# Two small constants move to a 96-byte pool at the top of SBUF, and every right-side pool starts 96 bytes lower

## The chip, the cores and the metric

The kernel runs on one core of a Trainium2 chip. The time is the device time of one execution in microseconds. The core has five engines that follow their own instruction lists and meet at semaphores: PE (TensorE, matrix products; its weight loads are listed apart as PEld), DVE (VectorE), ACT (ScalarE), POOL (GpSimd) and SP (SyncE, which here only issues DMAs). The on-chip memory, SBUF, has 128 partitions; a tile lies at the same byte address in each of its partitions. Products are collected in PSUM.

## The reference

One layer of a hybrid block over a sequence of 1024 tokens of width 1024, in float32: an input norm with a modulation, one wide input projection, a gated mixer (gMLP), a state-space mixer (SSD) with a short convolution, two output projections that are gated and merged, a last projection, a residual and a norm.

```
h = rms_norm(x, norm_w) * (1 + scale) + shift
gm_u, gm_v, gm_z, ssm_z, xbc, dt_raw, g_a, g_b = split(h @ w_in)          # 1024 x 11296
y_a = spatial_gating(gelu(gm_u), gelu(gm_v), ...) * silu(gm_z)
xs, bm, cm = split(silu(causal_conv(xbc)))
y_b = rms_norm_groups((ssd_scan(xs, softplus(dt_raw), ...) + xs * d_skip) * silu(ssm_z))
merged = sigmoid(g_a) * (y_a @ w_proj_a) + sigmoid(g_b) * (y_b @ w_proj_b)
out = rms_norm(x + gate * (merged @ w_out), final_norm_w)
```

## The kernel before

The products that need precision are made from operands split into a high and a low part of a 4-byte type (the profile prints it as f32 in a matmul and fp32r in a cast). One logical product is then three matmuls: high by high, high by low, low by high. Each of these matmuls takes 128 columns of weights and streams 512 columns past them. Where they occur, in order of time:

- **Input norm and first columns**, up to about 70 us: `first_products`, issued through the helper `mm` at line 76, results in `acc`.
- **Input projection**, about 70 to 930 us: `product` (line 556, its matmul at line 560). A 2x2 block scheme with seven products in place of eight (`pair`). Twelve matmuls in a row go to one PSUM bank; each has other weights than the one before it. The streamed operands are tiles of `hpool` (`b11`, `t1`, ...), the weights tiles of `wpool`.
- **SSD scan with the first output projection filled in**, about 930 to 1159 us: the SSD matmuls are plain float32 (`yi`, `yn`, `sp`, `pc`, `px`). Between them `proj_a` (line 1267) draws its matmuls, results in `pma`, six to twelve at a time; at the end a rest of them runs without SSD work in between. Each set of weights is used twice running, and the two uses go to two PSUM banks. All operands are tiles of `hpool`.
- **Second output projection**, about 1159 to 1325 us: `multiply` (line 1452, matmul at line 1459), 56 units of 12 matmuls in the order p1, p5, p2, p3, p6, p7, p4, eight units each. The streamed operands `bh` and `bl` are tiles of `hpool`. The weights (`p1a`, `p5a`, ...) come from `big` (line 1356), which takes tiles of the pools `p2r` and `p2q`. Three matmuls go to one PSUM bank, then three to the next. The operands of a unit are loaded six units ahead (`loads`) and made four units ahead (`operands`, lines 1419 to 1447) by ACT and DVE. SP issues the loads in an order that is written out, and waits before each until its tile is free.
- **Last projection**, about 1325 to 1402 us: `out_products` (matmul at line 1658). Its operands are placed by `place` (line 1474) in parts of `p2r`'s and `p2q`'s `sl` tiles or in `hpool` tiles, whichever is free. Some ten microseconds of norm, scaling and the last stores follow.

All instructions on PE are pinned in the order of the program; other engines' instructions are ordered by a scheduler when the kernel is built.

**Where tiles lie.** Pools are stacked from both ends of SBUF. Left, from low addresses: `const`, `hpool`, then `p0`, and after it `wpool` and `wspool`. Right, from the top down: `w4pool`, `gmpool`, `gxpool`, `prepool`, and for the later stages `p2r`, `p2x`, `p2q`. In the built program the right side ends at byte 229,344 of a partition, which is 96 above a multiple of 128. Its pools' sizes are multiples of 128 but for that of `gxpool`, the lowest of its stack, and so every tile of the pools named starts 96 above a multiple of 128, except in `gxpool`, whose tiles start at 64 or 0. `hpool` starts at 24,448 and its tiles and those of `wpool` all start at a multiple of 128. In the two projections at the end this gives, counted over the program's 512-column matmuls (start of the operand, modulo 128):

| matmul at line | count | streamed operand | weights |
|---|---|---|---|
| 560 | all | 0 | 0 |
| 76, `pma` | 384 | 0 | 0 |
| 76, `acc` | 108 and 36 | 0 and 96 | 0 |
| 1459 | 672 | 0 | 96 |
| 1658 | 53 | 0 | 0 |
| 1658 | 117 | 0 | 96 |
| 1658 | 147 | 96 | 96 |
| 1658 | 7 | 96 | 0 |

Of the kernel before, what the change touches and what calls it, by code (L numbers as in the profile page):

```python
# [8 lines left out]
F32 = mybir.dt.float32  # L9
# [7 lines left out]
P = 128  # L17
D = 1024
S = 1024
KT = D // P  # L20
NCH = S // P
NG = 8
# [13 lines left out]
def hybrid_kernel(  # L36
# [33 lines left out]
    def cst(shape, name, dt=F32):  # L70
        return const.tile(shape, dt, name=name, tag=name)

    pin = tc.keep_in_program_order

    def mm(acc, l, r, first=True, last=True):
# [35 lines left out]
    cwt = cst([P, P], "cwt")  # L111
    dtb = cst([P, NH], "dtb")
    abc = cst([P, NH], "abc")
    dskt = cst([P, 16], "dskt")
    dsk = cst([P, NH], "dsk")
    sc = cst([P, KT], "sc")
    dthq = cst([P, NCH * NH], "dthq")
    dde = cst([P, NCH * NH], "dde")
    nacs = cst([P, NCH * NH], "nacs")
    cd = cst([P, NCH * NH], "cd")  # L120
    ssq = cst([P, NG * NCH], "ssq")
    conv_wt = cwt.rearrange("p (k i) -> p k i", k=4)
    conv_bt = par2[:, 0:32]
    snw = par2[:, 32:48]
# [1670 lines left out]
```

## Time and profile before

| | |
|---|---|
| three runs | 1413.42, 1415.43, 1416.88 us (median 1415.43) |
| profiled execution, first to last instruction (its span) | 1412.0 us |
| profiled execution's own time | the page gives the span alone; the three runs lie 1.4 to 4.9 us above it |
| PE busy | 98% of the span |
| DVE, ACT, POOL busy | 75%, 56%, 15% |
| mean granted PE clock | 0.998 |

A row of a timeline gives the start, the time, the engine, the line and the operation with the tiles it writes and reads, and how many like instructions in a row it stands for. The end of a matmul is modelled in this profile, and matmuls overlap in it, so the pace of PE is read from starts: the difference of two rows' starts over the number of matmuls between them. A row of the chain of waits gives start, time and what held the end of the kernel at that moment. A row of a table by windows gives the window, its length, then busy time and number of instructions of PE, PEld, DVE, ACT and POOL, the granted clock, the DMA engines' busy share and GB/s.

### The profile page before, as it was taken

What the parts mean: (1) busy time and instruction counts of PE and PEld (TensorE: products, weight loads), DVE (VectorE), ACT (ScalarE), POOL (GpSimd) and SP (SyncE); (2) the same over time, 40 slices, a digit from 0 to 9 for tenths busy, and PEclk for the clock granted to TensorE, in tenths of its full rate; (3) what the DMA queues carried; (4) which work ended last, traced back from release to release, by engine and by line L of the source; (5) the groups of instructions that cost most, each with busy time, mean ns of one, the idle gap of its engine ahead of it and who ended that gap; (6) DMA issues with size and microseconds to landing.
All of it is one profiled execution on the core that took longest, in us unless ns stands there. A gap on an engine that the chain in (4) does not pass through costs nothing. (4 is left out here: it accounts for less than half of the span.)

```text
span 1412.0 us, 20661 instructions
## 1 busy us (share of the span) xinstructions
PE 1386.7 (98%) x7051; PEld 1147.0 (81%) x7051; DVE 1062.5 (75%) x1863; ACT 796.2 (56%) x1471; POOL 212.5 (15%) x208
## 2 busy tenths in 40 slices
PE   8999999999999999999999999999999999999997
PEld 7788888888888888887888888888888878777886
DVE  5686677767778899788888785388777767866866
ACT  6664575656656665555666555586766723322443
POOL 0000000000000011110100010027878830000001
PEclk9999999999999999999999999999999999999999
DMA  8552333343344667777675774498878759867903
GB/s 269 159 166 83 127 104 108 102 128 110 121 135 127 199 197 236 244 239 233 203 205 175 243 213 134 167 347 313 279 268 286 275 188 347 307 219 267 374 6 120
DMA packets 271918, 283.13 MB, mean 201 GB/s; under 512 B 14300, under 2 KB 222596, under 8 KB 271812
## 3 DMA queue, kind: packets, MB, share of 16 engines
q1 hardware_dynamic: 184548, 198.39, 44.0%
q10 hardware_dynamic: 87264, 83.41, 17.7%
q8 instruction: 56, 0.92, 0.3%
q14 instruction: 50, 0.41, 0.1%
HBM read 194.42 MB, written 87.33 MB: 200 GB/s over the span
## 5 line engine op out<-in xcount | busy, mean ns | idle before, releaser
L775 POOL TENSOR_TENSOR wog<-wog,gb 128x256 f32<-128x256 f32 x16 | 17.0, 1080 | 673.5 <-DMA wog<-in_w_out_dram 673.5
L989 ACT ACTIVATE dcy<-dcy,nacs 128x128 f32<-128x128 f32 x256 | 78.6, 389 | 15.2 <-POOL dcy L984 14.8
L984 POOL TENSOR_SCALAR_AFFINE_SELECT dcy<-dcy 128x1024 f32<-128x1024 f32 x32 | 35.0, 1094 | 138.2 <-ACT ea L981 134.6
L902 ACT ACTIVATE ac<-ac 128x1024 f32<-128x1024 f32 x32 | 33.9, 1060 | 25.9 <-DVE ac L900 25.8
L981 ACT ACTIVATE ea<-dcy 64x512 f32<-64x512 f32 x64 | 40.1, 626 | 14.7 <-DMA dcy<-acs_d 14.2
L76 PE MATMUL pma<-yh,wah 128*128 128x512 f32 x128 | 43.3, 419 | 0.0
L76 PE MATMUL pma<-yh,wal 128*128 128x512 f32 x128 | 42.6, 414 | 0.0
L1071 POOL TENSOR_TENSOR yz<-y,sl 128x512 f32<-128x512 f32 x32 | 41.5, 1296 | 1.1
L1009 DVE TENSOR_TENSOR dcy<-dcy,pc 128x1024 f32<-128x1024 f32 x32 | 38.9, 1216 | 2.9 <-PE pc L79 1.4
L1069 DVE TENSOR_TENSOR ym<-yn,ea 128x512 f32<-128x512 f32 (+1 forms) x32 | 19.9, 622 | 27.3 <-PE yn L76 27.3
L76 PE MATMUL pma<-yl,wah 128*128 128x512 f32 x128 | 40.2, 395 | 0.0
L1070 POOL TENSOR_TENSOR y<-y,ym 128x512 f32<-128x512 f32 (+1 forms) x32 | 36.6, 1143 | 12.0 <-DVE ym L1069 11.2
L76 PEld LDWEIGHTS yn<-sl,st 128*128 128x128 f32 x224 | 30.3, 190 | 7.0 <-POOL yz L1091 2.1
L76 PE MATMUL sp<-xe,bn 128*128 128x256 f32 x112 | 32.6, 408 | 3.2 <-DVE xe L1005 1.2
L900 DVE SCALAR_TENSOR_TENSOR ac<-c2x,cwt,ac 128x1023 f32<-128x1023 f32 (+2 forms) x24 | 31.2, 1299 | 5.8 <-ACT ac L898 5.7
L1398 DVE SCALAR_TENSOR_TENSOR yn<-yn,par,rb 128x512 f32<-128x512 f32 x32 | 23.9, 748 | 15.0 <-DMA yn<-yb_d 14.6
L76 PE MATMUL yi<-dcy,xd 128*64 128x128 f32 x512 | 35.0, 279 | 0.0
L76 PE MATMUL yn<-sl,st 128*128 128x128 f32 x224 | 31.3, 276 | 3.6 <-DVE st L1039 3.6
L900 DVE SCALAR_TENSOR_TENSOR ac<-c2cb,cwt,ac 128x1023 f32<-128x1023 f32 (+2 forms) x24 | 31.2, 1299 | 4.4 <-ACT ac L898 4.3
L1673 POOL TENSOR_TENSOR r<-r,fnw 128x512 f32<-128x512 f32 x2 | 2.6, 1300 | 209.3 <-DMA out_dram<-r 209.3
L1037 POOL TENSOR_TENSOR st<-st,cd 128x256 f32<-128x256 f32 x48 | 32.5, 678 | 8.2 <-PE yn L76 5.1
L900 DVE SCALAR_TENSOR_TENSOR ac<-c1cb,cwt,ac 128x1023 f32<-128x1023 f32 (+2 forms) x24 | 31.1, 1296 | 1.4 <-ACT ac L898 1.4
(2977 smaller groups left out, 4404.0 us busy)
## 6 DMA issues: line engine op xcount, KB each, us to landing
sl<-s_d SPq DMA_DIRECT2D x32, 768.0 KB, 4.7
s_d<-ac ACTq DMA_DIRECT2D x32, 512.0 KB, 4.2
dcy<-acs_d SPq DMA_DIRECT2D x32, 512.0 KB, 9.0
aw<-in_ada_w_dram SPq DMA_DIRECT2D x16, 512.0 KB, 3.7
wbr<-in_w_proj_b_dram SPq DMA_DIRECT2D x64, 128.0 KB, 4.4
wb_d<-wbb ACTq DMA_DIRECT2D x32, 256.0 KB, 4.9
wb_d<-wbc ACTq DMA_DIRECT2D x32, 256.0 KB, 4.1
yb_d<-yz ACTq DMA_DIRECT2D x32, 256.0 KB, 5.3
```

Source lines behind the costliest of these rows:

```text
L76: pin(PE.matmul(acc, l, r, start=first, stop=last))
L900: V.scalar_tensor_tensor(ac[:, s:], cc[:, : S - s], conv_wt[:, 3 - s, i : i + 1], ac[:, s:], op0=ALU.mult, op1=ALU.add)
L902: A.activation(ac, ac, AF.Silu)
L981: A.activation(ea[hh * HD : (hh + 1) * HD], dcy.rearrange("p (j e) i l -> p e j (i l)", e=2)[hh * HD : (hh + 1) * HD, hh], AF.Exp)
L984: G.affine_select(out=d8, in_=d8, compare_op=ALU.is_ge, fill=-1e30, base=0, pattern=[[0, 2 * HPG], [1, P]], channel_multiplier=-1)
L989: A.activation(dcy[:, h, i, :], dcy[:, h, i, :], AF.Exp, bias=sub[:, i, h : h + 1])
L1009: V.tensor_tensor(d3, d3, pc[:, 0:256].unsqueeze(1).to_broadcast([P, HPG, 256]), op=ALU.mult)
L1037: G.tensor_mul(v3(s2), v3(self.st), fac(cd, g, s)[:, i].unsqueeze(2).to_broadcast([P, HPG, HD]))
L1069: V.tensor_tensor(m[:, :, t0:], yn.rearrange("p (j l) -> p j l", j=2)[:, :, t0:], ea[:, :, t0:], op=ALU.mult)
L1070: G.tensor_add(y1[:, :, t0:], y1[:, :, t0:], m[:, :, t0:])
L1071: G.tensor_mul(yz, y1, sl[:, 4:6])
L1398: V.scalar_tensor_tensor(t, t, snw[:, n : n + 1], rbs[n // 2, h], op0=ALU.mult, op1=ALU.mult)
```

## The change

Two constants, `dskt` (64 bytes in a partition) and `sc` (32 bytes), leave the left `const` pool and become a pool of their own, `edge`, the first on the right side. `edge` takes the topmost 96 bytes, so every other right-side pool starts 96 bytes lower: 229,248 is now their upper end, a multiple of 128. `ssq` on the left gets 24 unused columns (96 bytes), so that `hpool` and all left pools behind it stay where they were.

```
+    edge = ctx.enter_context(tc.tile_pool(name="edge", bufs=1, side="right"))
+    def edg(shape, name):
+        return edge.tile(shape, F32, name=name, tag=name)
...
-    dskt = cst([P, 16], "dskt")
+    dskt = edg([P, 16], "dskt")
     dsk = cst([P, NH], "dsk")
-    sc = cst([P, KT], "sc")
+    sc = edg([P, KT], "sc")
...
-    ssq = cst([P, NG * NCH], "ssq")
+    ssq = cst([P, NG * NCH + 24], "ssq")
```

In the built program all engines have the same instructions in the same order as before, the DMAs included. Addresses move: the tiles of the right-side pools from 96 to 0 modulo 128 (those of `gxpool` from 64 or 0 to 96 or 32), and between `dsk` and `ssq` the constants `dsk`, `dthq`, `dde`, `nacs`, `cd` and `ssq` move down by 64 or 96 bytes, from 0 (`dsk`: 96) to 32. All 512-column matmuls of lines 560, 1459 and 1658, of `pma` and of `acc` then have both operands at 0. Since tiles of successive pools overlap at other edges, three waits are not needed any more: two semaphores of the first mask at line 984, one of a state update at line 1037, and one of a scaling at line 1005 (all at the start of the SSD stage).

## The prediction

> **What bounds the kernel now.** I read the page first, then the chain of waits, and then the timeline of PE, because a PE that is always busy can only get faster by its own pace.
>
> ```profile
> span 1412.0 us, 20661 instructions
> PE 1386.7 (98%) x7051; PEld 1147.0 (81%) x7051; DVE 1062.5 (75%) x1863; ACT 796.2 (56%) x1471; POOL 212.5 (15%) x208
> ```
>
> PE works 98% of the span, DVE 75%. An address can matter to the time only through PE, through the short stretches where PE waits, or by slowing another engine by a quarter. The chain in order of time, for the stages in which the change moves operands of matmuls:
>
> ```profile
> 1186.47 30.94 PE yp L1459 x132
> ...
> 1219.29 7.68 DMA yn<-yb_d
> ...
> 1236.46 20.65 PE yp L1459 x87
> 1257.12 42.18 PE x L1459 x180
> ...
> 1299.31 3.28 DMA p4a<-wb_d
> ...
> 1304.36 20.64 PE x L1459 x87
> 1325.00 11.09 PE ox L1658 x48
> 1336.09 11.15 PE oy L1658 x48
> 1347.24 33.43 PE ox L1658 x144
> 1380.67 19.53 PE oy L1658 x84
> 1400.21 1.44 PE ox L1658 x12
> ```
>
> These are runs of matmuls without a gap, so time over count is PE's own pace: 30.94/132 = 234.4 ns and 42.18/180 = 234.3 ns at line 1459; at line 1658 75.20 us over 324 matmuls (the first four rows), 232.1 ns. Between 1217.4 and 1236.5 us the chain leaves PE for a load and DVE, and between 1299.3 and 1304.4 us for another load.
>
> The same shape elsewhere, from the timeline of PE (three places: input projection, the end of `proj_a`, the first unit of the second projection):
>
> ```profile
> 849.72 1.07 PE L560 MATMUL yz<-t1h,p5z6h 128*128 128x512 f32 x4
> ...
> 861.51 1.07 PE L560 MATMUL zz<-b21l,p2z6h 128*128 128x512 f32 x4
> ```
> ```profile
> 1152.72 0.63 PE L76 MATMUL pma<-yl,wah 128*128 128x512 f32 x2
> ...
> 1154.57 0.62 PE L76 MATMUL pma<-yh,wal 128*128 128x512 f32 x2
> 1155.02 0.62 PE L76 MATMUL pma<-yh,wah 128*128 128x512 f32 x2
> ...
> 1158.65 0.62 PE L76 MATMUL pma<-yh,wal 128*128 128x512 f32 x2
> 1159.10 0.39 PE L1459 MATMUL x<-p1bh,p1a 128*128 128x512 f32 x1
> ...
> 1160.97 0.40 PE L1459 MATMUL x<-p1bh,p1a 128*128 128x512 f32 x1
> ```
>
> At line 560 thirteen groups of four take 11.79 us: 52 matmuls, 226.7 ns each. In the last stretch of `pma` eight groups of two take 1155.02 to 1158.65: 3.63/16 = 226.9 ns. With the very next matmul, the first of line 1459, the pace changes: 1159.10 to 1160.97 is eight matmuls, 233.8 ns. Before 1154.57, just after a break, `pma` ran 1.85/8 = 231.3 ns: after a break the pace needs some ten matmuls to come down.
>
> What differs between 226.9 and 233.8? The granted clock does not, nor the load on the DMA engines:
>
> ```profile
> 1154.50:1159.10 4.60, 4.60 (x21) 3.59 (x20) 1.00 1.05 395
> 1237.00:1299.00 62.00, 62.00 (x266) 49.82 (x265) 37.91 (x62) 16.05 (x26) 0.00 (x0) 1.00 0.75 251
> 1325.00:1401.00 76.00, 76.00 (x334) 61.64 (x333) 58.54 (x103) 34.56 (x73) 3.11 (x3) 1.00 0.32 122
> ```
>
> Windows (the first for line 76 alone, hence without DVE, ACT and POOL): clock 1.00 in all; the quick stretch has the busier DMA engines (1.05 against 0.75), and line 1658 is slow at 0.32. Reusing weights and changing the PSUM bank do not explain it either: `pma` does both, line 560 neither, and both reach 226.7 to 226.9. What remains is that at lines 560 and 76 both operands start at a multiple of 128 bytes, while line 1459 takes weights, and line 1658 weights or streamed columns, that start 96 above one. The first 48 matmuls of line 1658 have line 1459's order (three to a bank, weights used twice) and other starts, and run at 11.09/48 = 231.0 and not 234.3: the pace follows the addresses.
>
> **The change, part by part.** Counts and order of instructions stay on every queue, SP's and POOL's DMAs too; only addresses move.
>
> Second projection, line 1459: 672 matmuls go from starts (0, 96) to (0, 0). On the path are p1's 96, the row of 132, then 87, 180 and 87: 582. The other 90 run while the chain is on the two loads and DVE, and save nothing. I take 226.8 as the new pace (the mean of the two quick places): 582 x 7.5 ns = 4.37 us.
>
> Last projection, line 1658: 271 of 324 matmuls have at least one operand at 96 and all end at (0, 0). The stage runs without a break from 1304.4 on, so it can settle: 324 x (232.1 - 226.8) = 1.72 us. The 24 matmuls of 256 columns behind it (1.44 us for 12) I leave as they are; even at half of 5.3 ns each they would give 0.06 us.
>
> Breaks: after each, some ten matmuls run about 4.5 ns over the settled pace (231.3 against 226.8), 0.045 us. Four on the path (after 1160.97, before the row of 132, at 1236.46 and at 1304.36): 0.2 us off the gain.
>
> Cover: where PE gets quicker its operands must be ready 3% sooner. DVE has 37.91 busy of 62 us and 58.54 of 76 in the windows above. The load at 1219.29 was released by PE's progress (SP waits for a free tile), so it starts earlier by what PE saved and keeps its 7.68 us; the price if DMA does not follow is a rival below.
>
> Other matmuls: float32 ones show no such difference; the transposes that stream `x` (left, 0) and `sl` (right, 96) take
>
> ```profile
> L79 PE MATMUL px<-ident,x 128*128 128x128 f32 x64 | 10.0, 277 | 1.1 <-ACT hf L289 1.1
> L79 PE MATMUL px<-ident,sl 128*128 128x128 f32 x128 | 24.4, 273 | 0.0
> ```
>
> 277 and 273 ns, so the SSD stage gets nothing from PE, which I take as 0; bounds are 4 ns either way on these 128, 0.5 us. The 36 matmuls of `acc` with a streamed operand at 96 are broken up by transposes and never settle: 0, at most 36 x 5 ns = 0.2 us.
>
> ACT and DVE: the same cast and subtraction with tiles at 0 (`p5bh`, `p5bl`) and at 96 (`p2a`, `p2r`):
>
> ```profile
> L1437 ACT CAST p5bh<-yn 128x512 fp32r<-128x512 f32 x8 | 5.0, 625 | 10.8 <-DVE cwt L1113 5.5 <-PE x L1459 2.6 <-DVE yn L1429 2.4
> L1442 ACT CAST p2a<-p2r 128x512 fp32r<-128x512 f32 x8 | 5.0, 619 | 5.7 <-DMA p2r<-in_w_proj_b_dram 5.7
> L1438 DVE TENSOR_TENSOR p2bl<-yn,p2bh 128x512 fp32r<-128x512 f32 x8 | 5.5, 686 | 2.8 <-ACT p2bh L1437 2.7
> L1443 DVE TENSOR_TENSOR p2a<-p2r,p2a 128x512 fp32r<-128x512 f32 x8 | 5.5, 686 | 0.3 <-ACT p2a L1442 0.3
> L989 ACT ACTIVATE dcy<-dcy,nacs 128x128 f32<-128x128 f32 x256 | 78.6, 389 | 15.2 <-POOL dcy L984 14.8
> ```
>
> 625 and 619, 686 and 686 ns: no price for 96, so none is saved, and moving `dthq`, `dde`, `nacs`, `cd` and `ssq` from 0 to 32 costs nothing either. Their largest user is the exponential above; 6 ns (the spread of the casts) on all 256 would be 1.5 us, on an engine that is off the path. `dskt` and `sc` are scalar operands of a few instructions; 0. The three waits that go are at the stage's start, behind work that is done; 0, and at most a few tenths gained.
>
> Sum: 4.37 + 1.72 - 0.2 = 5.9 us. The profiled execution would span 1412.0 - 5.9 = 1406.1 us. The median of the runs lies 3.4 us above that execution's span, which I keep: 1415.43 - 5.9 = 1409.5 us, a ratio of 0.9958.
>
> A rule against this: the Trainium skill, page "SBUF — State Buffer", section "Specifications (TRN2)", gives SBUF lines of 16 bytes and a penalty for accesses that change lines too often. Starts of 96 and of 128 are both whole lines, so by that rule nothing changes and the sum is 0: 1415.4 us. The trace so far does not agree (226.9 and 233.8 ns in neighbouring matmuls).
>
> **The rivals.** *The pace belongs to the stage, not to the address.* Something that I haven't excluded (which bank or tile follows which, where instructions come from) sets 234 ns; then nothing moves: 1415.4 us. For it: no row has line 1459's order with both starts at 0. Against it: `pma`'s order and the first 48 of line 1658. The Trainium skill, page "TensorE: Matmul & The Clock Gate", section "Part 2: What happens when you issue a matmul", has the weight load and the streamed columns on two read ports of their own; by that the weights' start could not touch the spacing, and this rival would be right. Whether the trace agrees is what the change shows. 6 in 100.
>
> *It never settles.* Line 1459's pattern keeps the pace at that after a break, 231.3 ns: 582 x 3.0 + 324 x 0.8 = 2.0 us, 1413.4 us. For it: `pma` needs some ten undisturbed matmuls. Against: undisturbed runs here are 87 to 180 long. 7 in 100.
>
> *DMA becomes the bound of the second projection.* Up to 1205 us its engines are saturated (the row below), so the loads of p3 could come no sooner and 228 matmuls' 1.7 us would be lost, and 2 us more at 1299.3: 5.9 - 3.7 = 2.2 us left, 1413.2 us. For it the share of 1.03. Against it the next window: after that burst DMA stood idle, since SP waited for PE. 4 in 100.
>
> ```profile
> 1195.00:1205.00 10.00, 10.00 (x44) 8.07 (x43) 9.28 (x15) 5.19 (x9) 0.00 (x0) 1.00 1.03 382
> 1205.00:1210.00 5.00, 5.00 (x23) 3.99 (x23) 3.81 (x7) 3.38 (x6) 0.00 (x0) 1.00 0.08 23
> ```
>
> *Slower: equal starts collide.* Weights and streamed columns now begin at the same place modulo 128, and might hold each other up more than at different places. Each nanosecond on the 906 matmuls costs 0.9 us; it is slower by 0.3% from 4.7 ns more than now, 239 ns: 1419.7 us. Against it: `pma` and line 560 have equal starts and are the quickest. 3 in 100.
>
> **How the numbers follow.** The forecast holds 80 in 100, with a range of its own of 1407 to 1412 us: all 672 matmuls and fewer waits give up to about 7 us, a slower settling 4 us, and the medians of three runs scatter by one or two. The whole range reaches to the cases at 1413: 1406.5 to 1414. About 0.3%, 4.2 us, is what a measurement here can tell from no change: the forecast lies beyond it in 76 of its 80, which is faster 0.76; the rest of it and the first three rivals are same, 0.20; slower 0.04.
>
> **What would show it.** In the chain after, the long rows of line 1459 should read near 226.8 ns a matmul (180 in 40.8 us and not 42.18), those of line 1658 the same (144 in 32.7), with line 560, casts and subtractions unchanged. If line 1459 stays at 234, the address is not the cause; if it falls and the span doesn't, the two loads at 1219 and 1299 us have grown into waits of PE.

## The result and the profile after

The kernel with the change takes 1410.49 us (median of six runs, 1407.95 to 1411.57), the kernel before on the same chip 1417.64 us (six runs, 1413.42 to 1422.91). The ratio is 0.9942, with a 95% interval of 0.9922 to 0.9962. The forecast was 1409.5 us and a ratio of 0.9958, inside that interval. Part of the close landing in microseconds is chance: the kernel before turned out 2.2 us slower than the three runs shown, and the gain 1.3 us larger.

The page of the kernel after, head and first part:

```profile
span 1409.2 us, 20659 instructions
PE 1380.6 (98%) x7051; PEld 1146.3 (81%) x7051; DVE 1061.2 (75%) x1863; ACT 796.5 (57%) x1471; POOL 213.7 (15%) x208
```

That execution took 1411.01 us, 1.8 us more than its span. PE is still the bound, with 6.1 us less busy time. The lines of the kernel after stand five lines further down: 1464 is before's 1459, 1663 is 1658, 565 is 560. Its chain of waits in order of time, for the stages shown of before (start, time, what held the end):

```profile
1189.50 29.93 PE yp L1464 x132
...
1221.30 7.11 DMA yn<-yb_d
...
1237.90 20.02 PE yp L1464 x87
1257.92 40.93 PE x L1464 x180
1298.86 3.84 DMA p4a<-wb_d
...
1303.93 20.02 PE x L1464 x87
1323.95 10.88 PE ox L1663 x48
1334.83 10.88 PE oy L1663 x48
1345.71 32.64 PE ox L1663 x144
1378.35 19.04 PE oy L1663 x84
1397.39 1.45 PE ox L1663 x12
```

The row of 132 now reads 29.93/132 = 226.7 ns a matmul and not 234.4; that of 180 reads 40.93/180 = 227.4, with a short stall in it; the last projection 73.44/324 = 226.7 and not 232.1. The twelve of 256 columns are as before. In windows of the kernel after (window, length, busy time and count of PE, PEld, DVE, ACT, POOL, then clock, DMA share, GB/s):

```profile
1237.00:1299.00 62.00, 61.77 (x272) 50.62 (x271) 39.34 (x64) 16.23 (x27) 0.00 (x0) 1.00 0.75 254
1325.00:1400.00 75.00, 75.00 (x344) 62.59 (x342) 58.68 (x104) 35.41 (x76) 3.69 (x5) 1.00 0.31 120
```

In the same 62 us 272 matmuls start where 266 did, with the clock at 1.00 as before and the DMA share unchanged at 0.75.

Where the time of the two profiled executions went, stage by stage (the start, the SSD stage and the second output projection end where the next stage's first matmul starts, the input and the last projection where their own last matmul starts):

| stage, us | before | after | difference |
|---|---|---|---|
| start, to the first matmul of the input projection | 75.67 | 77.39 | +1.72 |
| input projection | 851.14 | 849.99 | -1.15 |
| SSD with `proj_a` | 232.30 | 234.71 | +2.41 |
| second output projection | 165.73 | 161.69 | -4.04 |
| last projection | 77.93 | 76.19 | -1.74 |
| tail | 9.25 | 9.24 | -0.01 |
| span | 1412.0 | 1409.2 | -2.8 |

The two stages that the forecast named gave 5.78 us; it had 5.9. The first three stages scatter from one execution to the next, which the runs below show.

### The profile page after: what moved, and what is told of

Same layout as the page of the kernel before. It is cut to its first block, busy times and chain, and to the rows that moved or that the text cites. A ratio compares the mean times of both kernels' runs of the same rounds, so it can differ in the third digit from the quotient of the medians.

```text
span 1409.2 us, 20659 instructions
## 1 busy us (share of the span) xinstructions
PE 1380.6 (98%) x7051; PEld 1146.3 (81%) x7051; DVE 1061.2 (75%) x1863; ACT 796.5 (57%) x1471; POOL 213.7 (15%) x208
```

## The experiments

The forecast rested on one sentence: that the pace is quick where both operands start at a multiple of 128. Three readings of it were to be told apart: each start by itself must be such a multiple; only the distance between the two starts matters; or the pace belongs to the stage. In what follows the distance is the start of the weights minus that of the streamed operand, in bytes; tiles of weights lie 512 apart, so it is fixed modulo 512. "Settled pace" is the mean spacing of the starts of 512-column matmuls that stand behind more than 16 others without a break (a spacing of some 260 ns or more); it is good to about 0.05 ns.

### The weights of the input projection moved alone

The input projection is the quick stage of the kernel before. A pad ahead of `wpool` moves its weights, and nothing else that a 512-column matmul reads (it is entered before `wpool` and left after it):

```
+    padpool = tc.tile_pool(name="padpool", bufs=1)
+    padpool.__enter__().tile([P, 24], F32, name="pad", tag="pad")
...
+    padpool.__exit__(None, None, None)
```

24 columns, 96 bytes:

> The kernel before, with 96 unused bytes between hpool and wpool while the input projection runs: its weights (line 560 of the kernel before) start at 96 modulo 128, its streamed columns still at 0; nothing else moves. If the starts set the pace, the settled spacing of the 3612 matmuls goes from 226.7 to 234.3 ns, the value of line 1459, and the input projection from 851 to about 878 us, the kernel from about 1415 to 1442 us. If the pace belongs to the stage, it stays at 226.7 ns and nothing changes.

16 columns, 64 bytes:

> As w96 with 64 unused bytes: weights at 64, streamed columns at 0. If the whole 128 bytes matter, the pace is above 226.7 ns, somewhere up to 234 ns (up to 27 us more). If only 64 do, it stays at 226.7 ns and the time at that of before. By the theory that the pace belongs to the stage also 226.7 ns.

8 columns, 32 bytes:

> As w96 with 32 unused bytes: weights at 32, streamed columns at 0. If the start within 64 bytes matters, the pace is that of w96, 234 ns, 27 us more. If the start matters in another way (distance to the next multiple of 128), it is another value above 226.7. By the theory that the pace belongs to the stage 226.7 ns, and the time of before.

Measured with 96 bytes: 1441.16 us (two runs), ratio 1.0161, interval 1.0110 to 1.0211, against 1417.67 us of the kernel before. With 64 bytes 1437.61 and with 32 bytes 1437.38 us (one run each). The timelines of PE give the pace; the two rows shown of each kernel are 13 groups of four, 52 matmuls, apart. First the kernel after, then 96, 64 and 32 bytes:

```profile
848.51 1.07 PE L565 MATMUL xz<-b11l,p1z6h 128*128 128x512 f32 x4
...
860.30 1.07 PE L565 MATMUL yz<-b22h,p3z6l 128*128 128x512 f32 x4
```
```profile
847.87 1.10 PE L562 MATMUL xz<-t3l,p7z5h 128*128 128x512 f32 x4
...
860.05 1.10 PE L562 MATMUL xx<-t2h,p6x7l 128*128 128x512 f32 x4
```
```profile
848.09 1.09 PE L562 MATMUL xx<-b11l,p1x7h 128*128 128x512 f32 x4
...
860.22 1.09 PE L562 MATMUL yx<-b22h,p3x7l 128*128 128x512 f32 x4
```
```profile
847.85 1.10 PE L562 MATMUL xx<-b11h,p1x7l 128*128 128x512 f32 x4
...
859.99 1.10 PE L562 MATMUL zx<-b21h,p2x7h 128*128 128x512 f32 x4
```

11.79/52 = 226.7 ns after, as before the change; 12.18/52 = 234.2 with 96 bytes, 12.13/52 = 233.3 with 64 and 12.14/52 = 233.5 with 32. So the rival "the pace belongs to the stage" falls: the same order of matmuls on the same banks takes line 1459's pace when its weights start 96 bytes on. The input projection got 23.96 us longer (851.14 to 875.10), the whole kernel 23.5 us. The settled pace on all 3612 matmuls of the line would be 3612 x 7.6 = 27.5 us. Of the 3.5 us between, 2.2 are fewer and shorter breaks: what the spacings of 300 ns and more in this stage take beyond 230 ns each sums to 6.7 us before and to 4.5 us with 96 bytes. The rest was not traced. The other stages keep their pace: 234.3 ns at line 1459 and 232.3 at line 1658 in all three.

### The streamed operand moved, the weights left

`hpool` starts 32 bytes lower, and a pad of 32 bytes keeps `wpool` where it was. The weights are then all at a multiple of 128, the streamed tiles at 96 above one; at line 1459 both are 96 above one, at a distance of 128.

```
-    dskt = cst([P, 16], "dskt")
+    dskt = par2[:, 64:80]
-    ssq = cst([P, NG * NCH], "ssq")
+    ssq = cst([P, NG * NCH + 8], "ssq")
...
+    padpool.__enter__().tile([P, 8], F32, name="pad", tag="pad")
```

> The other operand: hpool starts at 96 modulo 128 and wpool at 0, so the input projection streams from 96 against weights at 0; proj_a and both last projections then have both operands at 96. (dskt lies in an unused part of par2 for the room.) If only the weights' start matters, line 560 stays at 226.7 ns; if any operand off the multiple costs, it goes to 230 to 235 ns, 12 to 30 us more. Line 1459, with both at 96: 226.7 ns if the difference of the two starts matters, about 231 ns (the first 48 of line 1658 before) if each start does. By the theory that the pace belongs to the stage all stays as before.

Measured: 1435.63 us (one run, before 1417.67). Settled pace 233.34 ns in the input projection, 232.55 at line 1459. From the timeline of PE, again 52 matmuls:

```profile
848.14 1.10 PE L562 MATMUL xx<-b11l,p1x7h 128*128 128x512 f32 x4
...
860.27 1.10 PE L562 MATMUL yx<-b22h,p3x7l 128*128 128x512 f32 x4
```

12.13/52 = 233.3 ns. The streamed operand counts as much as the weights. And line 1459, where now no operand starts at a multiple of 128, got quicker by 1.7 ns and not slower: its distance had changed from 96 to 128. Neither of the values expected there (226.7 or about 231 ns) came. That a change of both starts moved the pace so little pointed from the starts to their distance.

### Everything at 96, and a distance of 160

If the distance decides, a kernel in which nothing starts at a multiple of 128 must be quick as long as both operands start alike. One line does it, since it lifts the left pools by 96 bytes to where the right side is:

```
-    ssq = cst([P, NG * NCH], "ssq")
+    ssq = cst([P, NG * NCH + 24], "ssq")
```

> The kernel before with the whole left side 96 bytes higher: both operands of every 512-column matmul at lines 560, 1459, 1658 and of pma start at 96 modulo 128. If only the difference of the two starts matters, all stages settle at 226.7 ns, the last two 6 us quicker than before. If each start matters, line 560 settles at 231 to 233 ns (232.6 at line 1459 in s96 with both at 96), the input projection at about 868 us, the kernel about 15 to 18 us slower than before.

The next one starts `hpool` 64 bytes lower than before and leaves `wpool`: a distance of 64 in the input projection and of 160 at line 1459.

```
-    dskt = cst([P, 16], "dskt")
+    dskt = par2[:, 64:80]
...
+    padpool.__enter__().tile([P, 16], F32, name="pad", tag="pad")
```

> hpool at 64 modulo 128 and wpool at 0: line 560 streams from 64 against weights at 0, pma has both at 64, line 1459 streams from 64 against weights at 96. If any start off a multiple of 128 costs, line 560 settles near 233.3 ns as with weights at 32 or 64, the input projection at about 872 us, the kernel some 20 us slower than before. If for the streamed operand 64 is enough, 226.7 ns and the time of before.

Measured: everything at 96 takes 1415.8 us, a distance of 64 and 160 takes 1437.22 us, before on the same chip 1418.26 us (one run each). The settled pace with everything at 96 is 226.67 ns in the input projection, 226.67 at line 1459 and 226.67 at line 1658. Its timeline of PE, and two rows of its chain of waits:

```profile
847.90 1.07 PE L560 MATMUL zx<-b21l,p2x7h 128*128 128x512 f32 x4
...
859.69 1.07 PE L560 MATMUL xx<-t4h,p4x7l 128*128 128x512 f32 x4
```
```profile
1262.88 38.15 PE x L1459 x168
...
1350.58 32.64 PE ox L1658 x144
```

11.79/52 = 226.7, and the 144 matmuls of line 1658 take 32.64 us, exactly as in the kernel after. So a multiple of 128 is not needed. With 64 and 160 the paces are 233.34 and 233.32 ns.

### Multiples of 128 at unequal distance

The opposite case: every start a multiple of 128, as in the changed kernel, but streamed operand and weights 128 apart modulo 256. Made from the changed kernel by moving three constants into unused columns of `par2`, so that `hpool` begins 128 bytes lower, with a pad ahead of `wpool` (the copy that fills `par2` then writes its first 64 columns alone):

```
-    dtb = cst([P, NH], "dtb")
+    dtb = par2[:, 88:120]
-    dskt = edg([P, 16], "dskt")
+    dskt = par2[:, 64:80]
-    sc = edg([P, KT], "sc")
+    sc = par2[:, 80:88]
+    edg([P, 24], "unused")
...
+    padpool.__enter__().tile([P, 32], F32, name="pad", tag="pad")
```

> The changed kernel with hpool 128 bytes lower (three more constants share the unused part of par2) and all other pools where they were: both operands still start at multiples of 128, but at different places modulo 256. If 128 is the step that matters, all stages settle at 226.7 ns and the time is that of the changed kernel, about 1410. If a larger step or the distance between the operands matters, the pace is another one, up to 234 ns and 27 us.

Measured: 1437.42 us (one run, before 1418.26). Settled pace 232.70 ns in the input projection, 232.89 at line 1459 and 231.75 at line 1658, while `pma`, whose operands both lie in `hpool`, stays at 226.63. From the timeline of PE and the chain of waits:

```profile
847.99 1.10 PE L568 MATMUL yx<-t1l,p5x7h 128*128 128x512 f32 x4
...
860.12 1.10 PE L568 MATMUL zx<-b21h,p2x7l 128*128 128x512 f32 x4
```
```profile
1281.31 41.92 PE x L1468 x180
...
1371.11 33.33 PE ox L1667 x144
```

12.13/52 = 233.3 (the mean over the stage is 0.6 lower), 41.92/180 = 232.9, 33.33/144 = 231.5: with every start at a multiple of 128 all three stages are slow. The rule of the forecast is refuted from both sides.

### The two halves of the change alone

The right side moved by an unused tile of 96 bytes, the first there, with `dskt` and `sc` left in `const` and no extra columns in `ssq`:

```
+    edge = ctx.enter_context(tc.tile_pool(name="edge", bufs=1, side="right"))
...
+    edg([P, 24], "unused")
```

> The change without its moved constants: an unused pool of 96 bytes at the top of the right side, dskt and sc stay in const, and dthq, dde, nacs, cd and ssq stay at 0 modulo 128. If the starts of the matmuls' operands are all there is, lines 1459 and 1658 settle at 226.7 ns and the ratio is that of the change, about 0.995 to 0.996. If the moved constants cost something in the SSD stage, this one is quicker than the change by that.

The constants moved in the same way (`dthq`, `dde`, `nacs`, `cd` and `ssq` 32 above a multiple of 128), the right side left at 96:

```
-    dskt = cst([P, 16], "dskt")
-    sc = cst([P, KT], "sc")
     ssq = cst([P, NG * NCH], "ssq")
+    dskt = cst([P, 16], "dskt")
+    sc = cst([P, KT], "sc")
```

> The constants alone: dskt and sc behind ssq, so that dthq, dde, nacs, cd and ssq start at 32 modulo 128 as in the changed kernel; the right side stays at 96. If the starts of the matmuls' operands are all there is, lines 1459 and 1658 stay at 234.3 and 232.2 ns and the ratio is 1.000 within 0.2%. If constants at 32 slow the SSD stage, it is above 1 by that.

The changed kernel a second time beside them:

> The changed kernel once more, beside the two halves of the change on one chip: a ratio of 0.994 to 0.997; the two halves' ratios multiply to it. The SSD stage was 2.4 us longer in its profile than in that of before; if that is scatter between executions, it is not there in every profile, and stays within 1 or 2 us of before on the average of the kernels.

Measured on one chip, against 1418.25 us of the kernel before (20 runs):

| kernel | runs | median, us | ratio | interval |
|---|---|---|---|---|
| right side alone | 9 | 1412.85 | 0.9961 | 0.9947 to 0.9975 |
| constants alone | 12 | 1417.37 | 1.0003 | 0.9988 to 1.0019 |
| the changed kernel | 6 | 1410.15 | 0.9945 | 0.9924 to 0.9965 |

Rows of the chains of waits at the second and the last projection: the right side alone, the constants alone, and the changed kernel again.

```profile
1261.67 38.20 PE x L1465 x168
...
1349.41 32.64 PE ox L1664 x144
```
```profile
1260.14 42.17 PE x L1459 x180
...
1350.33 33.43 PE ox L1658 x144
```
```profile
1254.62 38.18 PE x L1464 x168
...
1342.77 32.64 PE ox L1663 x144
```

With the constants alone the paces are before's (42.17/180 = 234.3, 33.43/144 = 232.2) and the time does not move. The right side alone has the new paces (38.20/168 = 227.4, 32.64/144 = 226.7) and 5.4 of the 8.1 us that the whole change gained beside it. The 2.7 us between are not accounted for; the two intervals overlap.

### A distance of 256, and everything at 96 in more runs

The kernel with a distance of 128, with `hpool` a further 128 bytes lower and a pad of 256 bytes ahead of `wpool`:

```
-    nhalf = cst([P, NCH], "nhalf")
+    nhalf = par2[:, 120:128]
-    ssq = cst([P, NG * NCH + 24], "ssq")
+    ssq = cst([P, NG * NCH], "ssq")
...
-    padpool.__enter__().tile([P, 32], F32, name="pad", tag="pad")
+    padpool.__enter__().tile([P, 64], F32, name="pad", tag="pad")
```

> As d128 with 256 in place of 128: hpool 256 bytes lower than in the changed kernel, everything else in place (four small constants share par2), so that streamed columns and weights start 256 apart modulo 512. If the distance counts modulo 256, all stages settle at 226.7 ns, the kernel at about 1410 us. If it counts modulo 512 or more, the pace is that of the other distances, 232 to 234 ns, and the kernel about 20 to 26 us slower. By the theory of the prediction (each start at a multiple of 128) 226.7 ns, which d128 has already refuted.

The second kernel is the one with everything at 96 (above), for a time with an interval:

> The kernel of a96 once more, timed: left and right side both at 96 modulo 128, so that streamed columns and weights are at distance 0 modulo 512 though no pool starts at a multiple of 128. If the distance is the cause, the last two stages are as in the changed kernel (226.7 ns, together 6 to 7 us shorter than before) and the ratio is the change's, 0.994 to 0.997. If tiles at 96 cost something of their own, as the 855 us of a96's input projection might say, the ratio is nearer 0.998 to 1.0.

Measured: 1414.17 us at a distance of 256 (one run), 1413.17 us with everything at 96 (12 runs), ratio 0.9966, interval 0.9949 to 0.9982, before 1417.77 us. The timeline of PE at a distance of 256:

```profile
848.72 1.07 PE L568 MATMUL xx<-t3l,p7x7h 128*128 128x512 f32 x4
...
860.50 1.07 PE L568 MATMUL xz<-t2h,p6z6l 128*128 128x512 f32 x4
```

11.78/52 = 226.5; settled 226.67 in all three stages. 256 bytes apart is as good as none. All settled paces of the study, by distance:

| distance, modulo 256 | ns a matmul | where |
|---|---|---|
| 0, equal starts at 0 modulo 128 | 226.6 to 226.8 | before, line 560 and `pma`; all stages after |
| 0, equal starts at 96 modulo 128 | 226.67 | everything at 96, all stages |
| 0, starts 256 apart | 226.67 | distance of 256, all stages |
| 32 | 233.3 | weights + 32; streamed - 32 (line 560) |
| 64 | 233.3 | weights + 64; streamed - 64 (line 560) |
| 96 | 234.3 | before, line 1459; weights + 96 (line 560) |
| 128 | 232.6 to 232.9 | streamed - 32 (line 1459); distance of 128 |
| 160 | 233.3 | streamed - 64 (line 1459) |

## Why the prediction was right, and where not

**The pace, and the two terms of the sum.** Right: the new starts made the matmuls quicker, by the forecast size. The last projection was to lose 1.72 us and lost 1.74; it takes 76.19 us in every kernel with a distance of 0. The second projection was to lose 4.37 - 0.2 = 4.17 us and lost 4.04 in the pair of profiles. Line 560, named as unchanged, is.

**The rule behind them failed.** The step that failed is "What remains is that at lines 560 and 76 both operands start at a multiple of 128 bytes". The rows that the forecast used fit it, because at lines 560 and 76 the two starts were also equal modulo 256. What the runs show in its place: the distance of the two starts, modulo 256, is 0 or it is not. For this change both rules foretell the same, since it makes the right side equal to the left; for other layouts they don't (all multiples of 128 and slow: 232.9 ns; none and quick: 226.67). That they agree here is luck: the new upper end of the right side, 229,248, and the start of `hpool`, 24,448, both leave 128 modulo 256, and the forecast looked at them modulo 128 alone. Had the right side moved down by 224 bytes and not by 96, also to a multiple of 128, the pace of the run at a distance of 128 gives, as an estimate, a gain of 582 x (234.3 - 232.9) ns = 0.8 us at line 1459 in place of 4.4.

**What the sum left out: PE waits a little more.** Over the six profiles with a distance of 0 the second projection takes 162.45 us on average (161.04 to 164.99), over the five in which line 1459 keeps its 234.3 ns 165.8 (165.08 to 166.54): 3.3 us gained and not 4.2. There the chain leaves PE for loads: in the changed kernel 7.11 us for `yn<-yb_d` and 3.84 for `p4a<-wb_d` (before 7.68 and 3.28). With the right side alone the first is longer, but so it is with the constants alone, at the old pace; when the changed kernel ran again another load came last. One row of each of these chains:

```profile
1225.90 8.31 DMA yn<-yb_d
```
```profile
1221.81 8.19 DMA yn<-yb_d
```
```profile
1293.24 5.73 DMA wlb<-wo_d
```

Summed over the stage, what two successive starts on PE lie apart beyond 440 ns is some 2.7 us (2.1 to 3.4) at the old pace and 3.7 (2.7 to 4.9) at a distance of 0. That a quicker PE waits more for its loads fits this, but the ranges overlap, so it is not shown. The rival "DMA becomes the bound of the second projection" is left with about 1 us at most, not the 3.7 it was priced at.

**The span.** 1406.1 us was forecast for a profiled execution and 1409.2 seen. The missing 3 us are the start and the SSD stage (+1.72 and +2.41, against -1.15 in the input projection), not the projections at the end. Those stages vary that much without any change to them: the SSD stage took 230.7 to 236.8 us over the kernels here, 234.7 and 230.7 in two executions of the changed kernel alone, the input projection at 226.7 ns 849.8 to 855.0. The second profile of the changed kernel spans 1406.3 us, but by a short SSD stage, so it does not confirm the sum either. The stages bear out a gain of 5 to 6 us, 0.4%; that the medians of the changed kernel show 7 to 8 is not accounted for; 0.4% still lies within their intervals.

**Costs put at nothing.** Right: the constants alone move the time by 0.03% (interval -0.12 to +0.19%). In the changed kernel the two casts shown of before take 624 and 621 ns (before 625 and 619), the two subtractions 686 and 685 (686 and 686) and the exponential 388 (389).

**The rivals.** "The pace belongs to the stage" is refuted by the weights moved alone. "It never settles" is refuted by the row of 132 at 226.7 ns. "Equal starts collide" has it the wrong way round: it is unequal starts that are slow, and 96 bytes more on one side of line 560 made the kernel 1.6% slower. The chances were added with a slip: 4 + 6 + 7 + 4 are 21 in 100 for no change and 3 for slower, not 20 and 4.

**The two rules weighed.** The trace does not agree with the first as it was used there: starts of 32, 64, 96 and 128 bytes are all whole lines of 16 bytes (the Trainium skill, page "SBUF — State Buffer", section "Specifications (TRN2)"), and yet cost 5.9 to 7.6 ns a matmul, depending on the other operand's start. Nor does it agree with what was drawn from the second (the Trainium skill, page "TensorE: Matmul & The Clock Gate", section "Part 2: What happens when you issue a matmul", two read ports of their own): moving nothing but the weights changed the spacing of the matmuls from 226.7 to 234.2 ns.

## What to carry to other kernels

Where 4-byte matmuls of 512 columns follow each other with new weights and PE is the bound, let weights and streamed operands start at the same place modulo 256; of the two places tried, 0 and 96 modulo 128, neither was quicker, and one line that pads the lower pool (24 unused columns) did the same to the pace as moving the upper pools. Look for it by the spacing of starts of the same shape in two stages of one trace: 226.7 against 233 to 234 ns was 3%, and 32 unused bytes ahead of one pool cost this kernel 20 us. When a rule is read from one trace, ask which other rule fits all the same rows, and build the layout in which the two differ.

## What was not expected of the hardware

That a distance between two addresses and not an address sets the pace, with a step and hardly a slope: 32 bytes already cost 6.6 of the 7.6 ns that 96 cost, 128 cost 5.9 to 6.2, 256 nothing. That 256 counts as 0 rests on one run. Why is open; no run looks inside the reading of the operands, nor tells whether a matmul's own weights count or those loaded for the next one. Distances of 192 and 224, steps under 32 bytes, other widths than 512 columns and other types were not tried.

At a distance of 0 the settled spacing is 226.67 ns, 680/3, in a pattern of three (227, 227, 226). After a break up to some eleven matmuls come before it, with spacings of 224 to 236 ns that follow much the same sequence in every kernel at this distance. At a distance of 96 the spacings repeat in sevens instead, 234, 235, 234, 231, 238, 237, 231 ns, 234.3 on average, at line 1459 of the kernel before and at line 562 with 96 bytes alike. What these patterns are is open.

So is the pace of line 1658 in the kernel before: with 200 of 324 matmuls at an equal start modulo 128 it still ran at 232.1 ns. The change moves all of the right side together, so it leaves the distance of two operands on the same side as it was; since all 324 run at 226.67 ns after it, those 200 were presumably at a distance of 0 modulo 256 before. A matmul at a distance of 0 among others that are not would then gain little by itself; no run tests that.
